# Scores of the two mixers: three products of rounded halves in place of one full-fp32 product

## The chip, the core and the metric

The kernel runs on one core of a Trainium2 chip. The metric is the time of one execution in device microseconds. Of the kernel before there are three runs: 2401.92, 2402.12 and 2405.55 us, a median of 2402.12. All times below are us unless marked ns. PE is the matrix engine (PEld its weight loads), DVE the vector engine, ACT the activation engine, POOL the general engine, and SP issues the weights' transfers.

## The reference

The model has two parts over one sequence of 256 tokens of width 1024. The first is a block of three attentions (block-sparse, dilated, memory), a gated merge and a convolved feed-forward. The second is a stack of two layers; each has a mixer and a layer of product-key experts (`peer`). The change is in the mixers alone. Cut to what matters there:

```python
h = rms_norm(x, norm1_g[l])
proj = h @ w_in[l]
q, k, v = ...                                   # 8 heads of 64
log_f = log_sigmoid(proj[..., F0:F1] + b_forget[l])
cum = cumsum(log_f)
logits = einsum("bhqd,bhkd->bhqk", q, k) * 64**-0.5
logits = logits + cum[q] - cum[k];  causal mask
y_att = softmax(logits) @ v
y_conv = silu(layer_norm(causal_dwconv(a * sigmoid(gate))))   # 31 taps
y_rnn = linear recurrence with gates, times gelu(gate_in)
x = x + concat(y_att, y_conv, y_rnn) @ w_out[l]
x = x + peer(rms_norm(x, norm2_g[l]), ...)
```

## The kernel before, in words

Weights come in as fp32 of 128x1024 (`wload`, L88). ACT rounds each to `hi` (fp32r, L102), and DVE or POOL makes the low half `lw` by a subtraction (L103). Activations are split in the same way (`split`, L106: ACT rounds, L108, and DVE subtracts, L109). A product of weights and activations is then three products of rounded halves, high x high, high x low and low x high: `gemm_n_unit` (L187, L188, L190; 512 columns) and `gemm_t` (L204 to L206; 256 columns). Attention is not done so: queries, keys, probabilities and values are plain fp32, and each of their products is one full-fp32 product, which the trace shows as two weight loads and two streams.

The mixer of layer `l` begins at L608. After the norm, the projections run as `proj_pair` (two weights into one PSUM tile of 512 columns). The queries and keys of heads 0 to 3 come first (`qk_proj`, L801) and ACT copies them to `qk` (L804); between the two projections stand the cumulative sum of the forget gates (L692, L693, which wait for `ff` of L678) and the recurrence's gates (L707). Then the values come (L822), and in the fill list the queries and keys of heads 4 to 7 (L841, L842) and the Gelu gate (L843).

`attention` (L224) is a generator in four stages for a pair of heads. Stage one makes the scores: for each half `t` of the queries and each head `j` one product L233 (64 rows, since a head is 64 wide; even heads sit in partitions 0 to 63, odd ones in 64 to 127), then `forget` adds the forget term (L814, bf16, 72 rows) and L238 adds the causal mask (bf16). For `t` = 0 a product has 128 columns, for `t` = 1 it has 256. Stage two: maximum (L248, DVE), Exp (L255, ACT), transposes (L274, PE), copies to SBUF (L276 ACT, L278 DVE). Stage three: the product with the values (L287) and the normalisation (L289). Stage four: transpose (L293) and split to `mh`, `ml`, the input of `w_out`.

`run_pairs` steps these generators in turn and puts fill between the stages: pairs 0 and 1 run together with the projections as fill, pair 2 with the first units of `w_out`, pair 3 (the last heads) with the other units. The convolution runs tap by tap on DVE (L732, `run_bg`), its layer norm is `ln_mean`, `ln_var`, `ln_out` (L759 to L790: L763, L773 and L786 on PE, L788 on DVE, then Silu on ACT, L789), and the recurrence is `rnn_roots`, `rnn_rsqrt`, `rnn_scan` (the long reciprocal is L741).

The order on each engine is not the order of the code: a scheduler places each instruction by its priority (`tc.high_priority`) and by when its inputs are expected. An engine then takes its instructions strictly in that order. An ACT function outside the loaded table needs an ACT_TABLE_LOAD, which stands in ACT's order too.

Of the kernel before, what the change touches and what calls it, by code (L numbers as in the profile page):

```python
# [10 lines left out]
F32 = mybir.dt.float32  # L11
F32R = mybir.dt.float32r
# [9 lines left out]
S = 256  # L22
# [28 lines left out]
def moba_peer_stack_kernel(ctx: ExitStack, tc: tile.TileContext, A, out):  # L51
    nc = tc.nc
    V, SC, GP, PE, SY = nc.vector, nc.scalar, nc.gpsimd, nc.tensor, nc.sync
# [52 lines left out]
    def split(hi, lo, ps, scale=None):  # L106
        if scale is None:
            SC.activation(hi, ps, AF.Copy)  # L108
            V.tensor_sub(lo, ps, hi.bitcast(F32))  # L109
        else:  # L110
            SC.activation(hi, ps, AF.Copy, scale=scale)  # L111
            V.scalar_tensor_tensor(lo, ps, scale, hi.bitcast(F32), op0=ALU.mult, op1=ALU.subtract)  # L112
# [111 lines left out]
    def attention(pool, heads, qT, kT, vv, full, dst, mask=None, cmul=None, extra=None):  # L224
        w0 = 256 if full else 128
        ws = [w0, 256]
        sp = [tmp_tile() for _ in range(2)]
        sps = [[sp[j][:, :w0] for j in range(2)], [sp[j][:, w0:w0 + 256] for j in range(2)]]
        for t in range(2):
            for j, h in enumerate(heads):  # L230
                o = sps[t][j]
                qs = qT(h)[:, t * 128:(t + 1) * 128]
                PE.matmul(o, qs, kT(h)[:, :ws[t]], start=True, stop=(full and extra is None))  # L233
                if extra is not None:
                    extra(o, h, ws[t])
                if not full:
                    if t == 0 or mask is None:
                        PE.matmul(o[:, t * 128:(t + 1) * 128], identb, trib, start=False, stop=True)  # L238
                    else:
                        PE.matmul(o, identb, mask, start=False, stop=True)  # L240
        yield
        mx = pool.tile([128, 2, 2], F32)
        for j in range(2):
            if full:
                V.tensor_reduce(mx[:, :, j], sp[j].rearrange("p (t k) -> p t k", t=2), axis=AX.X, op=ALU.max)
            else:
                for t in range(2):
                    V.tensor_reduce(mx[:, t, j:j + 1], sps[t][j], axis=AX.X, op=ALU.max)  # L248
        V.tensor_scalar(mx, mx, -SCALE, None, op0=ALU.mult)
        sm = pool.tile([128, 2, 2], F32)  # L250
        p = pool.tile([128, 2, 2, 256], F32)
        for t in range(2):
            for j in range(2):
                if cmul is None:
                    SC.activation(p[:, t, j, :ws[t]], sps[t][j], AF.Exp, scale=SCALE,  # L255
                                  bias=mx[:, t, j:j + 1], accum_out=sm[:, t, j:j + 1])
                else:
                    SC.activation(p[:, t, j, :ws[t]], sps[t][j], AF.Exp, scale=SCALE,
                                  bias=mx[:, t, j:j + 1])
                    V.scalar_tensor_tensor(p[:, t, j, :ws[t]], p[:, t, j, :ws[t]], 1.0,  # L260
                                           cmul[t], op0=ALU.mult, op1=ALU.mult,
                                           accum_out=sm[:, t, j:j + 1])
        V.reciprocal(sm, sm)
        on = pool.tile([128, 2, 2, 64], F32)
        pairs = [(k, t) for k in range(2) for t in range(2) if full or k <= t]
        n = len(pairs) * 128
        o0 = 0 if full else n
        ptss = []
        for j, h in enumerate(heads):
            pt = sp[j]  # L270
            pts = pool.tile([128, 512], F32)
            ptss.append(pts)
            for i, (k, t) in enumerate(pairs):
                PE.transpose(pt[:, i * 128:(i + 1) * 128], p[:, t, j, k * 128:(k + 1) * 128], ident)  # L274
            if j == 0:
                SC.copy(pts[:, :n], pt[:, :n])  # L276
            else:
                V.tensor_copy(pts[:, :n], pt[:, :n])  # L278
        yield
        for j, h in enumerate(heads):  # L280
            pt, pts = sp[j], ptss[j]
            ov = pt[:, o0:o0 + 128].rearrange("p (t d) -> p t d", t=2)
            for t in range(2):
                ks = [k for k in range(2) if (k, t) in pairs]
                for k in ks:
                    i = pairs.index((k, t))
                    PE.matmul(ov[:, t, :], pts[:, i * 128:(i + 1) * 128], vv(h, k),  # L287
                              start=(k == ks[0]), stop=(k == ks[-1]))
            V.tensor_mul(on[:, :, j], ov, sm[:, :, j, None].to_broadcast([128, 2, 64]))  # L289
        yield  # L290
        oT = sp[0]
        for t in range(2):
            PE.transpose(oT[:, t * 128:(t + 1) * 128], on[:, t].rearrange("p h d -> p (h d)"), ident)  # L293
        split(dst[0], dst[1], oT[:, :256])
# [34 lines left out]
    with ExitStack() as b1:  # L329
        ab = b1.enter_context(tc.tile_pool(name="b1", bufs=1))  # L330
# [276 lines left out]
    for l in range(L):  # L607
        with ExitStack() as mx:  # L608
# [20 lines left out]
            def proj_pair(i):  # L629
                ps = tmp_tile()  # L630
                for j in range(2):
                    wh, wl = wload(A["w2t"][l, 2 * i + j], 1024)
                    gemm_t(ps[:, j * 256:(j + 1) * 256], wh, wl, hh, hl)
                return ps.rearrange("p (a t) -> p a t", a=2)
# [161 lines left out]

            lo_on(GP)
            run_bg(8)
            qk = ab.tile([128, 8, S], F32)

            def qk_proj(i):  # L801
                for k in (0, 2):
                    s0 = 2 * i + 2 * k
                    SC.copy(qk[:, s0:s0 + 2], proj_pair(3 + i + k))  # L804
                    if k == 0:
                        forget_sum()
                        rnn_gates()
                    run_bg(10)

            def qf(s0):  # L810
                return lambda h: qk[(h % 2) * 64:(h % 2) * 64 + 64, s0 + h // 2, :]

            def forget(o, h, w):
                PE.matmul(o, sel[:, h, :], cumb[:, :w], start=False, stop=False)  # L814
# [12 lines left out]
            def pair_list(i, done):  # L827
                st = {}

                def unit(j):  # L830
                    if j == 0:
                        st["ps"] = acc_tile()
                    ps = st["ps"]
                    wh, wl = wload(A["w2t"][l, 2 * i + j], 1024)
                    gemm_t(ps[:, j * 256:(j + 1) * 256], wh, wl, hh, hl)
                    if j == 1:
                        done(ps.rearrange("p (a t) -> p a t", a=2))

                return [lambda: unit(0), lambda: unit(1)]

            fill = pair_list(4, lambda ps: SC.copy(qk[:, 2:4], ps))  # L841
            fill += pair_list(6, lambda ps: SC.copy(qk[:, 6:8], ps))  # L842
            fill += pair_list(7, lambda ps: SC.activation(gl, ps, AF.Gelu_apprx_tanh))  # L843
            fill = [lambda f=f: (f(), run_bg(12)) for f in fill]
            run_pairs([att(0), att(1)], fill, [2, 1, 1, 2], ahead=40)
# [325 lines left out]
```

## Time and profile before

| | |
|---|---|
| median of three runs | 2402.12 us |
| profiled execution | 2397.52 us |
| its span, first to last instruction | 2395.7 us |
| mean granted PE clock | 0.974 |
| PE busy | 2292.6 us, 96% |
| DVE / ACT / POOL busy | 67% / 52% / 28% |
| first mixer | 475 to 611 |
| second mixer | 1430 to 1566 |

The busy share counts a product until its modelled end, and products overlap, so durations on PE are not prices: the pitch between two starts is. The stretches in which the granted clock is 0.50 are given by the windows view. The two mixers are the same code with other weights, and their traces agree within a few tenths.

### The profile page before, as it was taken

To read this page: it belongs to the slowest core of one execution; us is meant where nothing else is said; L and a number is where in the kernel's file an instruction comes from. 1 tells how busy PE (TensorE), PEld (TensorE's weight loads), DVE (VectorE), ACT (ScalarE), POOL (GpSimd) and SP (SyncE) were. 2 spreads that over 40 slices of the span, in tenths; PEclk is the share of its full clock that TensorE was granted. 3 is DMA by queue.
4 is the path that set the end of the run, shared out by engine and by line. 5 is a ranking of instruction groups with operands and counts; after the bars stand their busy time and mean duration, and the time that the engine had idled before them with its cause. 6 is when DMAs were issued, how large, how long until landed. Compare 5 with 4: busy or idle time off the path is not lost. (4 is left out here: it accounts for less than half of the span.)

```text
span 2395.7 us, 37317 instructions
## 1 busy us (share of the span) xinstructions
PE 2292.6 (96%) x13972; PEld 2000.6 (84%) x13972; DVE 1611.9 (67%) x3269; ACT 1240.3 (52%) x1997; POOL 675.1 (28%) x279
## 2 busy tenths in 40 slices
PE   7799899989999999999999998999999999999998
PEld 6578688777898999998888877889899999888886
DVE  7832577767597667776666667759766777666665
ACT  5444466545444555555555544544455555555553
POOL 3436444334576111220000004468512122000000
PEclk9899899989999999999999998999999999999999
DMA  6424355524454555446666653445455555666664
GB/s 205 137 80 149 130 181 192 168 86 136 158 168 151 167 160 176 165 162 194 193 194 193 194 175 94 136 157 169 151 166 160 167 174 163 192 194 194 193 193 149
DMA packets 111934, 393.07 MB, mean 164 GB/s; under 512 B 13432, under 2 KB 14328, under 8 KB 111496
## 3 DMA queue, kind: packets, MB, share of 16 engines
q1 hardware_dynamic: 108288, 384.42, 50.6%
q10 hardware_dynamic: 3464, 6.26, 0.8%
q8 instruction: 110, 1.80, 0.3%
q14 instruction: 72, 0.59, 0.1%
HBM read 389.58 MB, written 1.05 MB: 163 GB/s over the span
## 5 line engine op out<-in xcount | busy, mean ns | idle before, releaser
L103 POOL TENSOR_TENSOR lw<-raw,hi 128x1024 fp32r<-128x1024 f32 (+1 forms) x275 | 674.9, 2459 | 1357.5 <-ACT hi L102 1159.4
L102 ACT ACTIVATE hi<-raw 128x1024 fp32r<-128x1024 f32 (+1 forms) x748 | 778.0, 1040 | 442.5 <-PE tmp L205 188.1
L103 DVE TENSOR_TENSOR lw<-raw,hi 128x1024 fp32r<-128x1024 f32 (+2 forms) x473 | 573.2, 1214 | 219.0 <-ACT hi L102 218.5
L204 PE MATMUL tmp<-th,hi 128*128 128x256 f32 x1696 | 494.6, 292 | 5.2 <-DVE th L112 3.3
L206 PE MATMUL tmp<-th,lw 128*128 128x256 f32 x1696 | 484.3, 286 | 9.8 <-POOL lw L103 9.8
L187 PE MATMUL acc<-hi,th 128*128 128x512 f32 x1248 | 491.0, 394 | 2.7 <-ACT pj L374 2.4
L188 PE MATMUL acc<-lw,th 128*128 128x512 f32 x1248 | 490.2, 393 | 2.6 <-POOL lw L103 1.9
L205 PE MATMUL tmp<-th,hi 128*128 128x256 f32 x1696 | 483.8, 285 | 0.3
L213 PE MATMUL tmp<-th,hi 128*128 128x512 f32 x1136 | 411.4, 399 | 0.9 <-DVE th L112 0.9
L190 PE MATMUL acc<-hi,th 128*128 128x512 f32 x1248 | 393.4, 391 | 0.0
L206 PEld LDWEIGHTS tmp<-th,lw 128*128 128x128 f32 x1696 | 327.4, 193 | 11.1 <-POOL lw L103 10.6
L204 PEld LDWEIGHTS tmp<-th,hi 128*128 128x128 f32 x1696 | 327.6, 193 | 8.0 <-DVE th L112 5.0
L205 PEld LDWEIGHTS tmp<-th,hi 128*128 128x128 f32 x1696 | 328.0, 193 | 1.2 <-DVE th L112 0.7
L187 PEld LDWEIGHTS acc<-hi,th 128*128 128x128 f32 x1248 | 235.8, 189 | 53.6 <-ACT pj L374 2.8
L188 PEld LDWEIGHTS acc<-lw,th 128*128 128x128 f32 x1248 | 236.1, 189 | 53.1 <-POOL lw L103 2.7
L215 PE MATMUL tmp<-th,lw 128*128 128x256 f32 x994 | 279.8, 281 | 0.0
L190 PEld LDWEIGHTS acc<-hi,th 128*128 128x128 f32 x1248 | 235.5, 189 | 49.6 <-issue 0.7
L111 ACT ACTIVATE th<-W 128x256 fp32r<-128x256 f32 x252 | 104.4, 419 | 284.5 <-PE acc L188 284.5
L213 PEld LDWEIGHTS tmp<-th,hi 128*128 128x128 f32 x1136 | 213.2, 189 | 41.8 <-DVE th L112 1.3
L215 PEld LDWEIGHTS tmp<-th,lw 128*128 128x128 f32 x994 | 188.9, 190 | 1.9
L112 DVE SCALAR_TENSOR_TENSOR th<-W,th 128x256 fp32r<-128x256 f32 x252 | 106.2, 424 | 111.5 <-PE acc L190 111.4
L982 DVE TENSOR_TENSOR tmp<-tmp,pb 128x256 f32<-128x256 f32 x98 | 42.4, 432 | 150.2 <-ACT pb L981 149.9
(339 smaller groups left out, 2472.1 us busy)
## 6 DMA issues: line engine op xcount, KB each, us to landing
raw<-in_u_dram SPq DMA_DIRECT2D x256, 512.0 KB, 3.7
raw<-in_v_dram SPq DMA_DIRECT2D x256, 512.0 KB, 3.5
raw<-in_w_up_dram SPq DMA_DIRECT2D x44, 512.0 KB, 3.6
raw<-in_w_in_dram SPq DMA_DIRECT2D x40, 512.0 KB, 3.5
raw<-in_w2t_dram SPq DMA_DIRECT2D x32, 512.0 KB, 3.9
raw<-in_wq_dram SPq DMA_DIRECT2D x32, 512.0 KB, 3.5
raw<-in_w_out_dram SPq DMA_DIRECT2D x24, 512.0 KB, 3.4
raw<-in_w_down_dram SPq DMA_DIRECT2D x22, 512.0 KB, 3.6
```

Of the source, the lines that this page charges most:

```text
L102: SC.activation(hi[:, :ncols], r, AF.Copy)
L103: lo.tensor_sub(lw[:, :ncols], r, hi[:, :ncols].bitcast(F32))
L111: SC.activation(hi, ps, AF.Copy, scale=scale)
L112: V.scalar_tensor_tensor(lo, ps, scale, hi.bitcast(F32), op0=ALU.mult, op1=ALU.subtract)
L187: PE.matmul(ps, lh, wh[:, sl], start=first, stop=False)
L188: PE.matmul(ps, lh, wl[:, sl], start=False, stop=False)
L190: PE.matmul(ps, ll, wh[:, sl], start=False, stop=last)
L204: PE.matmul(ps, wh[:, sl], ah[:, c, :], start=(c == 0), stop=False)
L205: PE.matmul(ps, wh[:, sl], al[:, c, :], start=False, stop=False)
L206: PE.matmul(ps, wl[:, sl], ah[:, c, :], start=False, stop=(c == KC - 1))
L213: PE.matmul(ps, wh[:, sl], a2[:, c].rearrange("p a b -> p (a b)"), start=(c == 0), stop=(c == KC - 1))
L215: PE.matmul(ps[:, :S], wl[:, sl], a2[:, c, 0], start=False, stop=False)
```

## The change

The score product takes its operands from two tiles, `qkh` (high) and `qkl` (low), both fp32r, which `split` fills from PSUM: ACT's copy becomes ACT's rounding and a DVE subtraction follows. In `attention`, three products of halves (high x high, high x low, low x high) accumulate where one full product stood. The first block's attentions pass single tiles and keep the full product.

```diff
@@ attention
-                qs = qT(h)[:, t * 128:(t + 1) * 128]
-                PE.matmul(o, qs, kT(h)[:, :ws[t]], start=True, stop=(full and extra is None))
+                q, k = qT(h), kT(h)
+                ts = slice(t * 128, (t + 1) * 128)
+                prods = [(q[a][:, ts], k[b][:, :ws[t]]) for a, b in ((0, 0), (0, 1), (1, 0))] \
+                    if isinstance(q, tuple) else [(q[:, ts], k[:, :ws[t]])]
+                for n, (qs, ks) in enumerate(prods):
+                    PE.matmul(o, qs, ks, start=(n == 0),
+                              stop=(n == len(prods) - 1 and full and extra is None))
@@ the mixers
-            qk = ab.tile([128, 8, S], F32)
+            qkh = ab.tile([128, 8, S], F32R)
+            qkl = ab.tile([128, 8, S], F32R)
+
+            def qk_split(s0, ps):
+                split(qkh[:, s0:s0 + 2], qkl[:, s0:s0 + 2], ps)
+
...
-                    SC.copy(qk[:, s0:s0 + 2], proj_pair(3 + i + k))
+                    qk_split(s0, proj_pair(3 + i + k))
...
-                return lambda h: qk[(h % 2) * 64:(h % 2) * 64 + 64, s0 + h // 2, :]
+                def at_head(h):
+                    r = slice((h % 2) * 64, (h % 2) * 64 + 64)
+                    return qkh[r, s0 + h // 2, :], qkl[r, s0 + h // 2, :]
+                return at_head
...
-            fill = pair_list(4, lambda ps: SC.copy(qk[:, 2:4], ps))
-            fill += pair_list(6, lambda ps: SC.copy(qk[:, 6:8], ps))
+            fill = pair_list(4, lambda ps: qk_split(2, ps))
+            fill += pair_list(6, lambda ps: qk_split(6, ps))
```

The scheduler also orders the mixers anew. In the changed kernel, L233 is L237, L238 is L243, L255 is L260, L276 is L281, L741 is L746, L743 is L748, L773 is L778, L789 is L794 and L814 is L827.

On PE, in the scores of the last pair of heads, this stood before (`qk` feeds the scores, `mh` and `ml` feed `w_out`):

```order
L233 MATMUL tmp<-qk 128x128
L814 LDWEIGHTS sel
L814 MATMUL tmp<-cumb,sel 128x128
L238 LDWEIGHTS identb
L238 MATMUL tmp<-trib,identb 128x128
L188 MATMUL acc<-lw,mh 128x512
L187 MATMUL acc<-hi,mh 128x512
L814 LDWEIGHTS sel
L814 MATMUL tmp<-cumb,sel 128x256
```

And this stands there now:

```order
L237 MATMUL tmp<-qkh 128x128
L187 MATMUL acc<-hi,mh 128x512
L237 MATMUL tmp<-qkl,qkh 128x128
L188 MATMUL acc<-lw,mh 128x512
L187 MATMUL acc<-hi,mh 128x512
L237 MATMUL tmp<-qkh,qkl 128x128
L188 MATMUL acc<-lw,mh 128x512
L827 LDWEIGHTS sel
L827 MATMUL tmp<-cumb,sel 128x128
L190 MATMUL acc<-hi,ml 128x512
```

Products of `w_out` have moved in between the three products of one score. Over this pair, from its first score to its last mask, 12 of them stand now and 7 stood before; between the last mask and the transposes of the probabilities 12 now and 9 before, between those transposes and L287 2 now and 8 before, and up to L293 3 now and 5 before.

On ACT, at the end of the mixer (the last pair's probabilities `p`, and the convolution's output `yc`), before:

```order
L255 ACTIVATE p,sm<-tmp,mx 128x128 x2
L255 ACTIVATE p,sm<-tmp,mx 128x256 x2
L102 ACTIVATE hi<-raw 128x1024
L789 ACT_TABLE_LOAD
L789 ACTIVATE yc<-yc,pv 128x256 x2
L276 COPY pts<-tmp 128x384
L108 ACTIVATE mh<-yc 128x512
```

Now:

```order
L794 ACT_TABLE_LOAD
L794 ACTIVATE yc<-yc,pv 128x256
L260 ACT_TABLE_LOAD
L260 ACTIVATE p,sm<-tmp,mx 128x128 x2
L260 ACTIVATE p,sm<-tmp,mx 128x256
L794 ACT_TABLE_LOAD
L794 ACTIVATE yc<-yc,pv 128x256
L260 ACT_TABLE_LOAD
L260 ACTIVATE p,sm<-tmp,mx 128x256
L108 ACTIVATE mh<-yc 128x512
L281 COPY pts<-tmp 128x384
```

The first Silu has moved ahead of the four Exp and the second between the third and the fourth, each with a table load on either side.

On DVE, ahead of the first scores, where the low half of the keys of heads 0 to 3 is made, now:

```order
L745 TENSOR_SCALAR rq<-th 128x512
L737 SCALAR_TENSOR_TENSOR acc<-yp,pv,acc 128x256
L746 RECIPROCAL rq<-rq 128x512
L109 TENSOR_TENSOR qkl<-tmp,qkh 128x512
L747 TENSOR_SCALAR av<-rq 128x512
L748 TENSOR_SCALAR tg<-th 128x512
```

The new subtraction stands right behind the reciprocal, where before the next steps of the recurrence stood. The other one for heads 0 to 3 (the queries) has taken the place of a tap two rows ahead of the last steps of `ff`. On POOL and SP nothing has moved.

## Rows read from the trace of the kernel before

**Rows 1.** The page, parts 1 and 4: busy time; the last chain's shares by engine.
```profile
PE 2292.6 (96%) x13972; PEld 2000.6 (84%) x13972; DVE 1611.9 (67%) x3269; ACT 1240.3 (52%) x1997; POOL 675.1 (28%) x279
...
PE 33%; POOL 0%; DVE 0%; ACT 0%; DVEq 0%; issue 0%; POOLq 0%; ACTq 0%
```

**Rows 2.** PE's waits, first mixer, 475 to 616: total, times, longest.
```profile
PE tmp L692 <- DVE ff L678: 6.4, 1, 6.4
...
PE tmp L233 <- ACT qk L804: 1.1, 1, 1.1
PE acc L206 <- POOL lw L103: 0.8, 1, 0.8
```

**Rows 3.** PE in order of time, scores of pair 2: start, duration, engine, line.
```profile
566.68 0.28 PE L205 MATMUL acc<-th,hi 128*128 128x256 f32 x1
566.80 0.28 PE L206 MATMUL acc<-th,lw 128*128 128x256 f32 x1
567.01 0.48 PE L233 MATMUL tmp<-qk 64*128 64x128 f32 x2
567.42 0.39 PE L204 MATMUL acc<-th,hi 128*128 128x256 f32 x1
...
569.45 0.70 PE L233 MATMUL tmp<-qk 64*128 64x256 f32 x2
570.07 0.38 PE L204 MATMUL acc<-th,hi 128*128 128x256 f32 x1
```

**Rows 4.** PE in order of time, from the last pair's last mask on.
```profile
591.32 0.33 PE L238 MATMUL tmp<-trib,identb 128*128 128x128 bf16 x1
...
593.47 0.39 PE L187 MATMUL acc<-hi,mh 128*128 128x512 f32 x1
593.70 0.39 PE L188 MATMUL acc<-lw,mh 128*128 128x512 f32 x1
...
594.84 0.82 PE L274 MATMUL tmp<-ident,p 128*128 128x128 f32 x6
595.41 0.71 PE L190 MATMUL acc<-hi,ml 128*128 128x512 f32 x2
...
598.17 1.55 PE L287 MATMUL tmp<-vn,pts 128*128 128x64 f32 x12 [0.65 <-ACT pts L276]
...
600.76 0.38 PE L293 MATMUL tmp<-ident,on 128*128 128x128 f32 x2
```

**Rows 5.** ACT and DVE in order of time: copies, reciprocal and subtraction of 128x512.
```profile
526.69 3.34 DVE L741 RECIPROCAL rq<-rq 128x512 f32<-128x512 f32 x1
...
530.59 0.57 ACT L804 COPY qk<-tmp 128x512 f32<-128x512 f32 x1
...
598.02 0.63 ACT L108 ACTIVATE mh<-yc 128x512 fp32r<-128x512 f32 x1
...
599.35 0.68 DVE L109 TENSOR_TENSOR ml<-yc,mh 128x512 fp32r<-128x512 f32 x1
```

**Rows 6.** ACT (and one DVE row) in order of time, behind the last scores.
```profile
593.03 0.36 ACT L255 ACTIVATE p<-tmp,mx 128x128 f32<-128x128 f32 x1
...
593.38 0.47 ACT L255 ACTIVATE p<-tmp,mx 128x256 f32<-128x256 f32 x1
...
594.80 0.75 DVE L788 TENSOR_TENSOR yc<-yc,tmp 128x256 f32<-128x256 f32 x2 [1.44 <-PE tmp L786]
...
595.36 1.28 ACT L789 ACT_TABLE_LOAD   x1
596.66 1.09 ACT L789 ACTIVATE yc<-yc,pv 128x256 f32<-128x256 f32 x2
597.66 0.46 ACT L276 COPY pts<-tmp 128x384 f32<-128x384 f32 x1
```

**Rows 7.** Windows: stretch, length, busy (count) of PE, PEld, DVE, ACT, POOL; granted clock, DMA.
```profile
514.70:524.90 10.20, 6.29 (x19) 4.57 (x20) 9.98 (x32) 1.93 (x5) 0.00 (x0) 0.50 0.12 33
586.40:593.20 6.80, 6.80 (x19) 4.05 (x19) 3.46 (x18) 0.59 (x4) 0.00 (x0) 0.50 0.50 158
```

## The prediction

> **What bounds the kernel now.** I read the page's first and fourth parts first, then PE's waits in the first mixer, then PE and ACT in order of time where the scores are made. PE is busy 96% of the span, and the chain that ended last is PE's wherever its steps are named [rows 1]. So time that PE gains or loses in a mixer is kept, unless PE waits there for something else. In the first mixer it waits 6.4 us for the forget gates (DVE), 1.1 us for the ACT copy of keys at the first scores, 0.8 us for one low weight half from POOL, and 0.65 us at L287 for the last heads' probabilities [rows 2, 4]. The second mixer repeats the pattern.
>
> The scores are small: 2 mixers x 4 head pairs x 2 heads x 2 query halves = 32 products with 64 rows. What matters is what stands around one. The L206 product at 566.80 streams for 0.12, as the pitch from 566.68 shows, so it ends at 566.92; the score product starts at 567.01, 0.09 later, and the next L204 starts 0.41 after that [rows 3]. For 256 columns instead of 128 the 0.41 becomes 0.62: 128 columns more cost 0.21, so 128 columns stream for 0.21 and 0.20 is fixed (a weight load of about 0.11 with nothing beside it, and 0.09 before the next row count). The L204 behind it then takes 0.39 where others take 0.28: another 0.11 for its own weights [rows 3]. **A visit to the 64-row form costs 0.09 + 0.11 + 0.09 + 0.11 = 0.40 us beside its streaming**, and about 0.29 where a bf16 mask (L814) follows, whose weights load faster. Full fp32 alone isn't the reason: six full-fp32 transposes with 128 rows and the step to the next product take 0.57 together, under 0.10 each [rows 4].
>
> **The change part by part.**
>
> *Products on PE.* Each score product of full fp32 becomes three rounded ones. Counted in PE's order, a visit is a run of score products with nothing else between. Per layer there were 14 visits (6 end at a mask), now 24 (8 end at a mask): the scheduler puts other products between the three. Before: 6 x 0.29 + 8 x 0.40 = 4.9. After: 8 x 0.29 + 16 x 0.40 = 8.7. So +3.8 per layer. Streaming: 8 products of 0.21 and 8 of 0.42 were 5.0; now 24 of 256 columns at 0.12 (the pitch of the same form with 128 rows) are 2.9, and 24 of 128 columns cost between 0.06, half of that, and 0.11, if the weight load sets the pitch. I take 0.08, since some stand alone and some follow one another: 1.9. Streaming changes by -0.2 (-0.7 to +0.5). PE: **+3.6 per layer**.
> No row shows a rounded product with 64 rows. Its ends are the streaming alone, with no price for the visit (the first rival), and the 0.62 of a full product each; I take the measured price of the visit, which its neighbours pay whatever the type.
>
> *The first scores.* They waited for L804 [rows 2]. Now ACT's rounding copy takes about 0.06 more (0.63 against 0.57), and the low part is a DVE subtraction of 0.68 behind it [rows 5]. Three products of high parts can run meanwhile, some 0.3. A subtraction also stands in place of one conv tap ahead of the forget gates' last steps, for which PE waits anyway: 0.2. So 0.06 + 0.68 - 0.3 + 0.2 = **+0.65 per layer**. On DVE the subtraction of the keys stands behind the long reciprocal of L741, which ended at 530.03, before ACT's copy began at 530.59, so it waits for ACT and not for DVE; behind it stand the steps of the recurrence, whose end is needed only much later.
> A layer's other two subtractions, for the heads 4 to 7, lie beside PE's streaming of other weights: 36 products at 0.12 stand in PE's order between the transposes that go before them on ACT and the first score that wants a low half. Without that cover they would cost up to 0.63 + 0.68 = 1.3 each; I cost them at nothing.
>
> *The last heads.* Here ACT's order matters more. Before, the four exponentials of the last pair stood together and the convolution's two Silu after them, with one table load. Now Silu and Exp alternate: Silu, three Exp, Silu, one Exp, with a load of 1.28 ahead of each, three more per layer. From the last mask at 591.32 to L287 at 598.17 it took 6.85 us [rows 4]. After: the first convolution multiply on DVE (about 0.4) and its semaphores (about 0.4), then on ACT load 1.28, Silu 0.50, load 1.28, Exp 0.35 + 0.35 + 0.47, load 1.28, Silu 0.50, load 1.28, Exp 0.47, the rounding copy of yc 0.53, the copy of probabilities 0.46: 8.75 [rows 5, 6]; with the lead 9.5, of which 0.2 run before the last mask: 9.3, or +2.5. Then two products of w_out fewer stand between L287 and L293 (0.23 each [rows 4]), so L293 comes **+2.0 later** after the last score. PE cannot hide it, since 14 products and the transposes (some 4 us) stand in the 9.3. Five products of w_out that used to fill this time now stand ahead of the last score: 5 x 0.23 = **+1.15**.
>
> *What is absorbed.* The 0.8 wait for POOL lies behind the first scores, so lateness up to there can vanish in it, if POOL isn't late itself; its weights wait for buffers that PE frees. Between 0 and 0.75; I take 0.4.
>
> *The clock.* PE's granted clock is 0.50 (1.2 GHz) between 586.4 and 593.2, in the midst of the last scores and without a wait ahead of it; it is 0.50 too from 514.7, in the 6.4 us wait, to 524.9 [rows 7]. I take the stretch at the last scores to stay as long as it is. If it went, each layer would gain back about 2.4, half of the 4.9 from 586.4 to the last mask; if one more of 6.8 us fell on dense work, it would cost half, 3.4.
>
> *Sum.* Per layer 3.6 + 0.65 + 2.0 + 1.15 - 0.4 = 7.0; two layers +14.0. The profiled execution took 2397.5 (2395.7 of span and 1.8 around it), so 2411.5 by it. The median of the runs is 4.6 above that execution; on the median the forecast is **2416 us**.
>
> **The rivals.**
> *The price belongs to the full-fp32 product, not to the row count.* Then the 28 visits of before lose 28 x 0.40 = 11.2, streaming gives 0.4, and the waits and moved work of the two layers add 2 x (0.65 + 2.0 + 1.15 - 0.4) = 6.8: 2402.1 - 11.6 + 6.8 = 2397, faster. It decides at the 64-row runs. Against it: transposes and L287 of full fp32 pay no such gap [rows 4], and the gap stands on both sides of the 64-row product. The Trainium skill (TensorEngine Tiling (Array Packing), Tiling Modes) says that a change of tiling mode drains the engine; the 0.09 on either side agrees. Chance 0.07.
> *The tail and the fragments are hidden.* If Exp and Silu find time while PE has work after all, and the visits overlap because the two heads sit in different row halves, half of the 14 stays: 2404 to 2409. For it: the order puts the two heads' products side by side at the first scores. Against: 128-row products stand between most visits, and at the last pair ACT has nothing but its own chain to do. Chance 0.13.
> *The clock falls longer.* The last scores have 11 visits instead of 4, and behind them PE would wait some 5 us; the 6.4 us wait went with half speed [rows 2, 7]. One more stretch per layer gives 2416 + 6.8 = 2423, two 2430. Chance 0.22.
> *A switch of tables costs more than its load.* If ACT had to run empty at each switch and that took as long as the load, the four of the chain would add 2 x 4 x 1.28 = 10: 2426. Against it: Silu follows 0.02 after the load's end [rows 6]. The Trainium skill (ScalarE: Activation LUTs, What ACT_TABLE_LOAD costs) gives about 2.66 us for a switch, 1.28 of it the load and the rest a drain, by which it would be 11; the row's 1.28 agrees for the load, and no drain shows in it. Chance 0.01.
>
> **How the numbers follow.** The forecast holds 0.57 (2410 to 2420). About 0.2%, 4.8 us, is what a measurement of this kernel can tell from no change. The first rival is faster, or in part the same: faster 0.05, same 0.02; of the second about half lies under 2406.9: same 0.07; slower 0.86. The range leaves out the first rival's end and the two-stretch end: 2404 to 2427.
>
> **What would show it.** The products of L237 are 96 in the mixers, and each visit in the last scores still has 0.09 ahead and 0.4 around it. L794 and L260 have three more table loads per layer, and PE waits about 5 us for the last pair's probabilities where it waited 0.65. The wait at the first score gets some 0.7 longer in all. PE's gaps elsewhere (before L165 and L204) stay. I am wrong if rounded products follow 128-row ones without a gap, if the last wait stays under 2 us, or if the difference lies outside the two mixers.

## The result: slower, 2434 us, and the profile after

The changed kernel takes 2433.68 us (2432.20 to 2433.75) against 2402.12, a ratio of 1.0128, 95% interval [1.0109, 1.0146]. Run once more later it took 2435.14, 1.0131 [1.0105, 1.0158]. I had said 2416 and at most 2427: the direction was right, the size was not. The loss is 31.6 us, where I had 14.

The page's parts 1 and 4 read as before [rows 1], PE's chain first:

```profile
PE 2317.0 (95%) x14004; PEld 2016.3 (83%) x14004; DVE 1614.0 (66%) x3277; ACT 1247.6 (51%) x2003; POOL 672.1 (28%) x279
...
PE 33%; POOL 0%; DVE 0%; ACT 0%; issue 0%; DVEq 0%; POOLq 0%; ACTq 0%
```

Where the time went is best read between marks that both traces have. Starts of PE's products in the first mixer, counted from its first L165, and by how much each comes later after the change (the second mixer in the last column):

| mark (line after) | before | after | later | later, second mixer |
|---|---|---|---|---|
| first score (L237) | 51.34 | 51.48 | +0.1 | -1.3 |
| statistics of the convolution (L768), w_out under way | 96.36 | 96.92 | +0.6 | -0.6 |
| last score (L237) | 109.20 | 121.03 | **+11.8** | **+10.8** |
| last pair's L292 | 118.30 | 132.72 | +14.4 | +13.4 |
| last pair's L298 | 120.90 | 136.57 | +15.7 | +14.6 |
| next stage (L165) | 135.49 | 151.52 | +16.0 | +15.0 |

The two mixers lose 31.0 together. What lies outside differs too, without a changed instruction in it: the first mixer began 7.1 us later in this profile, and 1.8 came back elsewhere. Over all kernels of this study, that start lay between 0.1 and 13.4 us behind the one of before, 9.9 in the second profile of the same changed kernel; so stages are compared from the mixer's start, and a total within some microseconds by medians only.

Of the 11.8, 11.3 arise between L768 and the last score, and so do 11.4 in the second mixer. The mark L768 is not quite steady: seven products of `w_out` stood ahead of it before, three stand there now, and each takes 0.23. A steadier stretch is that from the last pair's first score, which has 24 products of `w_out` ahead of it in every kernel here, to its last mask: 17.81 now (591.48 to 609.29), 7.26 before (584.06 to 591.32). Of this difference 1.5 are the third pair's L292, which stands behind that first score now and stood ahead of it before.

The windows of the changed kernel (stretch, length, busy time and count of PE, PEld, DVE, ACT, POOL, then granted clock, DMA share, GB/s) answer to [rows 7]:

```profile
593.60:614.10 20.50, 19.64 (x47) 11.75 (x47) 6.19 (x25) 5.69 (x11) 2.87 (x2) 0.50 0.24 78
617.50:624.30 6.80, 6.17 (x23) 5.55 (x24) 3.05 (x6) 2.53 (x6) 0.00 (x0) 0.50 0.00 1
1563.00:1583.50 20.50, 19.65 (x47) 11.75 (x47) 6.19 (x25) 5.68 (x11) 2.87 (x2) 0.50 0.24 78
```

In both mixers PE runs at half clock (1.2 GHz) for 20.5 us where it was 6.8 [rows 7], and again for 6.8 us behind its wait in the tail. The rows of PE in order of time show visits to the 64-row form at the full clock (first pairs and third pair), and what they become in the stretch:

```profile
547.85 0.38 PE L237 MATMUL tmp<-qkh 64*128 64x256 f32 x1
548.16 0.51 PE L190 MATMUL acc<-hi,th 128*128 128x512 f32 x1
548.59 0.39 PE L237 MATMUL tmp<-qkh 64*128 64x256 f32 x1
...
575.39 0.28 PE L206 MATMUL acc<-th,lw 128*128 128x256 f32 x1
575.60 0.32 PE L237 MATMUL tmp<-qkh 64*128 64x128 f32 x1
575.85 0.39 PE L204 MATMUL acc<-th,hi 128*128 128x256 f32 x1
...
594.73 0.69 PE L298 MATMUL tmp<-ident,on 128*128 128x128 f32 x2 [0.86 <-DVE on L294]
...
600.59 0.58 PE L237 MATMUL tmp<-qkh 64*128 64x256 f32 x1
601.10 0.79 PE L187 MATMUL acc<-hi,mh 128*128 128x512 f32 x1
601.82 0.58 PE L237 MATMUL tmp<-qkl,qkh 64*128 64x256 f32 x1
602.33 0.79 PE L188 MATMUL acc<-lw,mh 128*128 128x512 f32 x1
603.06 0.58 PE L237 MATMUL tmp<-qkh,qkl 64*128 64x256 f32 x1
603.57 0.79 PE L187 MATMUL acc<-hi,mh 128*128 128x512 f32 x1
```

At the full clock the rounded product starts 0.09 behind the end of L206 (575.39 + 0.12), the next starts 0.25 later and takes 0.39 instead of 0.28: just the visit that I had priced for the full fp32 product [rows 3], and with a rounded one it is the same. A score of 256 columns and one product of 512 columns take 0.74 together at the full clock (547.85 to 548.59) and 1.23 in the stretch (600.59 to 601.82), so half clock costs this mixture 0.4 of its time, not half. The last two heads made four visits before; now they make eleven, with twelve products of w_out between them instead of seven.

PE's waits from 482 to 624 (total, times, longest) answer to [rows 2]:

```profile
PE tmp L697 <- DVE ff L683: 6.5, 1, 6.5
...
PE tmp L279 <- ACT p L260: 3.2, 1, 3.2
...
PE tmp L237 <- ACT qkh L108: 1.1, 1, 1.1
PE tmp L298 <- DVE on L294: 0.9, 1, 0.9
PE acc L206 <- POOL lw L103: 0.5, 1, 0.5
PE tmp L237 <- DVE qkl L109: 0.3, 1, 0.3
```

The 3.2 at L279 took the place of 0.65 at L287, and 0.9 at L298 (for the third pair, at 594.73 above) is new. ACT's own rows in the tail show why the first is there, answering to [rows 6]:

```profile
609.82 1.28 ACT L794 ACT_TABLE_LOAD   x1 [1.86 <-DVE yc L793]
611.12 0.60 ACT L794 ACTIVATE yc<-yc,pv 128x256 f32<-128x256 f32 x1
611.72 1.28 ACT L260 ACT_TABLE_LOAD   x1
613.02 0.37 ACT L260 ACTIVATE p<-tmp,mx 128x128 f32<-128x128 f32 x1
...
614.30 1.28 ACT L794 ACT_TABLE_LOAD   x1
615.60 0.60 ACT L794 ACTIVATE yc<-yc,pv 128x256 f32<-128x256 f32 x1
616.21 1.28 ACT L260 ACT_TABLE_LOAD   x1
617.51 0.47 ACT L260 ACTIVATE p<-tmp,mx 128x256 f32<-128x256 f32 x1
```

Silu and Exp alternate, four loads of 1.28 where there was one. From the last mask at 609.29 to L292 at 619.68 it took 10.4, against 6.85 [rows 4].

### The profile page after: what moved, and what is told of

Its sections match the earlier page's. It is cut to its first block, busy times and chain, and to the rows that moved or that the text cites. A ratio compares the mean times of both kernels' runs of the same rounds, so it can differ in the third digit from the quotient of the medians.

```text
span 2432.0 us, 37389 instructions
## 1 busy us (share of the span) xinstructions
PE 2317.0 (95%) x14004; PEld 2016.3 (83%) x14004; DVE 1614.0 (66%) x3277; ACT 1247.6 (51%) x2003; POOL 672.1 (28%) x279
## 5 line engine op out<-in xcount | busy, mean ns | idle before, releaser
L206 PE MATMUL tmp<-th,lw 128*128 128x256 f32 x1696 | 482.1, 284 | 9.8 <-POOL lw L103 9.8
L206 PEld LDWEIGHTS tmp<-th,lw 128*128 128x128 f32 x1696 | 325.1, 192 | 11.1 <-POOL lw L103 10.6
```

The lines of the kernel that those rows point to most:

```text
L206: PE.matmul(ps, wl[:, sl], ah[:, c, :], start=False, stop=(c == KC - 1))
```

## The experiments

Theory: the single 64-row products among the last heads' 128-row ones hold PE at half clock, and that is what I missed. Rivals: the order of the last pair does it, whatever the rows; the visits alone; ACT's tail; the rounding and its splits. Ratios are to the kernel before, run on the same chip beside each group: 2400.1 (first four), 2400.2 (next four), 2404.9 (last three).

**All scores with 128 rows.**
```
- qkh = ab.tile([128, 8, S], F32R)
+ kh = ab.tile([128, 4, S], F32R)
+ qzh = ab.tile([128, 4, 2, S], F32R)
...
+     V.memset(z[(1 - r) * 64:(2 - r) * 64, :, r, :].bitcast(F32), 0.0)
...
+     split(qzh[p, s0:s0 + 2, r], qzl[p, s0:s0 + 2, r], ps[p])
```


> The changed kernel, but a head's query lies in 128 rows with its other 64 set to zero, and its key comes with the neighbour's: all 96 rounded products of the scores have 128 rows, and the order on every engine is that of the changed kernel; the same scores are computed. Clock theory (in each mixer the last pair's stretch at half speed, 20.5 us, comes from the 64-row products standing singly among 128-row ones): the gaps around them go (24 x 0.4 us a layer) and the stretch is as short as before the change, 6.8 us; 2434 - 2 x (9.6 + 7) is about 2401, and with the dearer splits 2400 to 2410. Order theory (the longer half-speed stretch comes from the order and the waits of the last pair, whatever the rows): the gaps go, the stretch stays over 15 us, 2414 to 2420. Tail theory (the ScalarE chain behind the last mask costs most): over 2420.

Measured 2424.11, 1.0086 [1.0061, 1.0112]. Between L768 and the last score the loss fell from 11.3 to 2.5 and 2.7, and the stretch there to 6.8 us (600.2 to 607.0): the clock theory's signs. But the order did not stay as I had meant: 14 products of w_out stand ahead of L768 here, three in the changed kernel, so 2.5 of that gain (11 x 0.23) are the mark's. From the last pair's first score to its last mask, over the same products in nearly the same order, it is 11.22 (597.80 to 609.03) instead of 17.81. The time is far above the clock theory's 2400 to 2410. The 13 visits of the first three pairs are gone, yet w_out begins 96.1 us into the first mixer, as in the changed kernel (96.2), because PE waits 3.3 us more for ACT and DVE there; that the splits by halves of rows cause these waits is likely and not shown. The tail stayed (1.9 up to L292, 1.25 to L298), and this profile began its first mixer 13.4 late.

**The last pair in full fp32.**
```
+ if s0 % 4 == 2:
+     split(qkh[:, s0:s0 + 1], qkl[:, s0:s0 + 1], ps[:, :1])
+     SC.copy(qkf[:, s0 // 4:s0 // 4 + 1], ps[:, 1:])
...
+ if h >= 6:
+     return qkf[r, s0 // 4, :]
```


> The changed kernel, but the scores of the last two heads of each mixer (6 and 7) are full fp32 products again, from an unsplit copy: 4 visits to the 64-row form instead of the many single ones in the last pair, ScalarE's tail (Silu and Exp in turn) as in the changed kernel. Clock theory: the half-speed stretch at the last scores is back at 6.8 us, and what is left over the kernel before is the tail (about 4 us a layer), the first score (under 1) and a few visits (1 to 1.5): 2402 + 2 x 6 to 7, so 2412 to 2417. Visits theory (the stretch is not the cause, only the 0.4 us of each visit): 3 visits a layer less, 2434 - 2.4, about 2431. Tail theory: 2430 or more, since the tail is unchanged.

Measured 2434.07, 1.0138 [1.0117, 1.016]: far from what my theory said. But the edit moved the order as well: the third pair, still rounded, now stands singly among the products of the gate, ten visits instead of six, and there the clock fell:

```profile
574.90:585.10 10.20, 10.20 (x35) 7.95 (x36) 3.28 (x10) 1.31 (x2) 2.34 (x1) 0.50 0.25 84
...
595.40:605.60 10.20, 9.99 (x29) 6.34 (x29) 4.77 (x22) 1.25 (x2) 0.00 (x0) 0.50 0.34 104
```

Up to L768 6.0 us are lost in the first mixer, and 7.5 in the second, that weren't lost in the changed kernel. It doesn't decide between the theories; it shows that the place isn't bound to the last pair, and that an experiment has to hold the order. It also speaks against a simple count of visits: the last pair makes four, as before the change, and its stretch is 10.2, not 6.8.

**Silu behind the last Exp.**
```
+ def ln_silu():
+     for c in range(2):
          SC.activation(yc[:, c], yc[:, c], AF.Silu, scale=P(f"lg{l}", c), bias=P(f"lb{l}", c))
      split(mh[:, 4:6], ml[:, 4:6], yc)
...
- run_pairs([att(3)], units[4:7], 1, ahead=40)
+ run_pairs([att(3)], [lambda: None, lambda: (ln_silu(), units[4]()), units[5]], 1, ahead=40)
+ units[6]()
```


> The changed kernel, but the Silu of the gate is emitted behind the Exp of the last heads, so ScalarE changes its table 29 times in the program instead of 31, and the last heads' probabilities come without a change between them; the products of the scores stay as they are and stand singly among the products of w_out (22 visits a layer instead of 24). Tail theory: the time from the last mask to the last products of the probabilities falls from 10.4 us to about 7.5; 2434 - 2 x 3 to 4, so 2426 to 2428, more if the chain is most of the loss. Clock theory: the stretch of 20.5 us at half speed stays, 2425 to 2431; if the stretch falls below 10 us here, the time is under 2420 and neither the rows nor the single visits were what set it.

Measured 2426.09, 1.0108 [1.0085, 1.0131]. That fits both theories' times. The scheduler still put one Silu ahead of the Exp, so the probabilities still waited for two loads; the tail up to L292 stayed 2.2 above before, and my edit tested that theory only in part. Of the 3.4 us a layer that it gained, 2.9 came between L768 and the last score, where two visits and three products of w_out fewer stood and the stretch was 17.1 in both mixers.

**No w_out between the last scores.**
```
-         lambda: (ln_out(), units[3]()), lambda: None]
+         lambda: ln_out(), lambda: None]
...
- run_pairs([att(3)], units[4:7], 1, ahead=40)
+ def behind_scores():
+     with tc.issue_after(last_mask["m"].ins):
+         units[3]()
+ run_pairs([att(3)], [lambda: (behind_scores(), units[4]()), units[5], units[6]], 1, ahead=40)
```


> The changed kernel, but the twelve products of w_out that stand between the last pair's scores are issued behind the pair's last mask, so nothing of 128 rows comes between the last scores but the decay's two products, the masks and the transposes; 20 visits a layer instead of 24, the rounded 64-row products as they are, and the tail's wait filled with products of w_out; table changes 25. Clock theory: the scores themselves are over in about 8 us instead of 20; if the mixture with w_out's products held the clock down, the stretch is 10 us or less and the time is 2434 - 2 x (7 + 1.6 + 2 to 4), so 2408 to 2414. Rows theory (64-row products hold the clock down whatever lies between): the stretch moves with the scores and stays as long for w_out's products behind them; 2420 to 2428. Tail theory: the wait for the probabilities is filled, 2434 - 2 x 4, so about 2426.

Measured 2401.85, 1.0011 [0.9996, 1.0027]: nearly all of the loss is gone, with the same rounded 64-row products. The windows of the two stretches:

```profile
588.30:598.50 10.20, 10.20 (x33) 7.16 (x33) 5.08 (x23) 2.10 (x9) 0.56 (x1) 0.50 0.33 104
1544.00:1554.20 10.20, 10.20 (x33) 7.16 (x33) 5.09 (x23) 2.10 (x9) 0.57 (x1) 0.50 0.33 104
```

They are 10.2 us instead of 20.5. From L768 to the last score, with as many products of w_out between as before, it is 1.6 longer than before, and Exp stands together again, so PE no longer waits for it: L292 follows the last score only 0.7 later than before. The time is below every forecast. The two mixers give back 26.8 of the 32.3 us between the two profiled executions, a little over the 25 that the clock theory had at most; 5.2 lie ahead of the first mixer, where nothing differs.

**128 rows for the last pair alone.**
```
+ if s0 == 2:
+     split(qkh[:, 2:3], qkl[:, 2:3], ps[:, :1])
+     for r in range(2):
+         p = slice(r * 64, r * 64 + 64)
+         split(qzh[p, r:r + 1], qzl[p, r:r + 1], ps[p, 1:])
...
+ if h >= 6:
+     return (qkh[:, 7, :], qkl[:, 7, :]) if s0 else (qzh[:, h - 6, :], qzl[:, h - 6, :])
```


> The changed kernel, but of the last two heads of each mixer alone (6 and 7) the query lies in 128 rows with the other 64 zero; PE's order is that of the changed kernel, product for product, and the same scores are computed. Clock theory: between the start of w_out and the last score the loss falls from 11.3 us a layer to the 2.5 of the kernel with 128 rows throughout, and the half-speed stretch from 20.5 us to 6.8; 2434 - 2 x 8.8, so 2414 to 2419. Order theory (the stretch belongs to the order of the last pair, whatever the rows): the stretch stays over 15 us and only the visits go, 10 x 0.4 us a layer: 2426 or more.

Measured 2420.32 (2413.90 to 2422.45), 1.008 [1.0056, 1.0104], just above the clock theory's range and below the order theory's; the profiled execution took 2413.9. From the last pair's first score on PE's order is that of the changed kernel, product for product; a few products of the gate and of L768 ahead of it stand elsewhere. The window of the last scores:

```profile
586.70:595.50 8.80, 7.42 (x54) 6.27 (x53) 6.80 (x21) 2.33 (x4) 2.35 (x1) 1.00 0.38 121
```

And PE's rows of the same products as shown above of the changed kernel:

```profile
590.11 0.44 PE L298 MATMUL tmp<-ident,on 128*128 128x128 f32 x2 [1.38 <-DVE on L294]
...
592.48 0.28 PE L237 MATMUL tmp<-qkh,qzh 128*128 128x256 f32 x1
592.61 0.40 PE L187 MATMUL acc<-hi,mh 128*128 128x512 f32 x1
592.84 0.29 PE L237 MATMUL tmp<-qkl,qzh 128*128 128x256 f32 x1
592.96 0.39 PE L188 MATMUL acc<-lw,mh 128*128 128x512 f32 x1
593.20 0.28 PE L237 MATMUL tmp<-qkh,qzl 128*128 128x256 f32 x1
593.31 0.40 PE L187 MATMUL acc<-hi,mh 128*128 128x512 f32 x1
```

Same order, and now the clock is 1.00 through all the last scores: a score and a w_out product take 0.36 (592.48 to 592.84) instead of 1.23. From the first score of the pair to its last mask it is 8.63 us (586.79 to 595.42) where the changed kernel needs 17.81 (591.48 to 609.29). From L768 to the last score the loss is 1.8 and 2.0 instead of 11.3 and 11.4, of which 0.9 are four products of w_out that stand ahead of the mark here. That excludes the order by itself, and the rounding: in this order it is the row count of 24 products, 12 a layer. (With 64 rows the order counts too, as the run without w_out between the last scores shows.) The half-speed stretch did come later (602.5 to 612.7), in the tail behind PE's wait, which is still there (5.3 us at L279). Of the 8 us a layer that are left, 6.2 lie behind the last mask and 1.7 and 2.0 ahead of it, where five products of w_out and four of L791 stand that stood behind it before.

The kernel with 128 rows throughout has the same products in its last pair and took 11.22 for them, with 6.8 us at half clock, where this one took 8.63 with none. So 6.8 us at half clock cost 2.6 there, again 0.4 of it. And since neither has a 64-row product there, the row count doesn't explain why a stretch of 6.8 begins in the one and none in the other.

**The kernel before, no w_out between the scores.** The edit of the fourth run, full fp32.

> The kernel before the change, with w_out's products moved behind the last pair's last mask as in the run without w_out between the scores, the full fp32 products left. If the move only takes away what the change added, it does nothing here: 2398 to 2402. If it also fills the wait of 5 us for the last heads' probabilities, which the kernel before has too: 2 x 2 to 4 us faster, 2392 to 2397. The difference from the changed kernel with the same move (2401.9) is the price of the rounded products by themselves: by the visits (6 more a layer at 0.4 us) and the first score (0.7), 2 x 3.1, about 6 us.

Measured 2394.51, 0.9977 [0.9963, 0.9991]: faster than before, at the time of the second reading but not for its reason: the kernel before waits 0.65 for the last heads' probabilities [rows 4], not 5. In the profile the mixers end 0.9 and 3.7 earlier than before's, but they stand 1.6 and 1.4 ahead at the first score already, where nothing is edited yet; and in the second mixer the stretch is 3.4 instead of 6.8. What made this kernel faster is not shown. Against 2401.85 with rounded products, these cost 7.3 us in this order (I had said about 6), the longer stretch included.

**Grouped, no w_out between.**
```
+ for a, b in ((0, 0), (0, 1), (1, 0)):
+     for j, h in enumerate(heads):
+         PE.matmul(sps[t][j], q[a][:, ts], k[b][:, :ws[t]], start=(a + b == 0), stop=False)
```


> The changed kernel with w_out's products behind the last scores, and in addition the products of the two heads of a pair issued in turn, all high by high, then the cross products: 14 visits to the 64-row form a layer, as many as before the change, instead of 20. Visits theory: 2401.9 - 2 x 6 x 0.4, about 2397. If the clock alone counts, and it is as good as it gets already: 2400 to 2403. Over 2405 if the first score's wait for both heads' splits costs more than the visits give.

Measured 2398.97, 0.9993 [0.9979, 1.0007]; 2.9 of the expected 4.8 us came. The intervals of the two runs overlap, and the stretch is shorter too, 6.8 us with five visits in the last scores, so this doesn't price the visits by themselves. By its median it is the best form of the rounded scores here, the same as the kernel before, and 4.5 us behind it with the same move.

**The changed kernel again.**

> The changed kernel itself once more, as a control: 2431 to 2437. If the half-speed stretch of 20.5 us in the last scores is the same at every execution, it is 17 to 21 us here in both mixers; if it was an accident of one profile, it is shorter in one of them. The time until the first mixer, in which nothing is changed, lay 7.1 us apart in the two profiles; if that is chance, it lies elsewhere here.

Measured 2435.14, and the stretches to the digit:

```profile
597.00:617.50 20.50, 19.64 (x47) 11.75 (x47) 6.17 (x25) 5.70 (x11) 2.87 (x2) 0.50 0.24 78
1566.40:1586.90 20.50, 19.66 (x47) 11.72 (x47) 6.22 (x25) 5.64 (x10) 2.92 (x2) 0.50 0.25 78
```

They are no accident of a profile. The start of the first mixer is: 9.9 us behind before's here, 7.1 in the first profile.

**The kernel before, each score cut in three.**
```
- PE.matmul(o, qs, kT(h)[:, :ws[t]], start=True, stop=(full and extra is None))
+ for c0, c1 in zip(cuts, cuts[1:]):
+     PE.matmul(o[:, c0:c1], qs, kT(h)[:, c0:c1], start=(c0 == 0), stop=(full and extra is None))
```


> The kernel before the change, full fp32 scores without any split, but each score's product is cut into three along the keys (44, 44 and 40 columns, and 88, 88 and 80): as many products as in the changed kernel, and on PE the last pair in nearly the changed kernel's order, single products of 64 rows between w_out's of 128; 28 visits a layer. If it is the breaking up of the scores that costs (visits and clock) and not the rounding: a half-speed stretch of 15 us or more at the last scores, and 2420 to 2440. If it is something in the rounded products or in the split: the stretch stays near 6.8 us, and only the visits (14 more a layer at up to 0.4 us) and ScalarE's order show: 2400 to 2416.

Measured 2443.66, 1.0175 [1.0152, 1.0199]: full fp32 scores, nothing rounded, and slower than the changed kernel. The time fits the breaking up of the scores, but the clock fell elsewhere than I said: not at the last scores, but 10.2 us long at the third pair (from 576.2), as in the run with the last pair in full fp32, and again in the tail:

```profile
576.20:586.40 10.20, 10.20 (x38) 8.27 (x38) 3.73 (x11) 0.85 (x1) 2.34 (x1) 0.50 0.18 51
613.70:623.90 10.20, 8.30 (x28) 7.20 (x29) 3.57 (x7) 4.06 (x7) 0.00 (x0) 0.50 0.13 36
```

Part of the loss is the pieces themselves, 4.3 us by the first pair's transposes, and 10.9 of the 21.5 us a layer are lost by the last pair's first score, where the changed kernel had lost next to nothing. So a loss of this size needs no rounding, but it is not the same loss. The last pair makes nine visits here, between the same products as in the changed kernel, and the clock is 1.00 throughout: 11.58 from its first score to its last mask (595.13 to 606.71). That speaks against the theory that the visits alone set the stretch; its place I can't foretell.

**The kernel before, no w_out between, and 128 rows for heads 4 to 7.**
```
+ def q_pad(ps):
+     for r in range(2):
+         p = slice(r * 64, r * 64 + 64)
+         SC.copy(qz[p, :, r], ps[p])
...
+ if h >= 4:
+     return qk[:, s0 + h // 2, :] if s0 else qz[:, h // 2 - 2, h % 2, :]
```


> The kernel before the change with w_out's products behind the last scores (2394.5), and in addition the queries of the last four heads of each mixer in 128 rows with the other 64 zero, full fp32: half of the scores need no change of form. By the visits (7 of 14 a layer go, 0.3 to 0.4 us each): 2394.5 - 2 x 2 to 2.8, so 2389 to 2391. If the copies by halves of rows or the zeros cost as much as that: 2394 to 2398.

Measured 2390.56, 0.9946 [0.9927, 0.9965], the fastest: 11.6 us under the kernel before by its first median, 14.4 by its runs beside. Its interval and that of the same kernel without the 128 rows just touch. In the profile the mixers end 4.8 and 5.9 earlier than before's, of which 1.6 and 1.2 stand at the first score already. In the last scores and behind them the clock stays full:

```profile
583.50:604.00 20.50, 19.29 (x112) 15.93 (x112) 9.88 (x34) 10.40 (x20) 7.05 (x3) 1.00 0.35 104
```

**Grouped alone.** The edit of the seventh run, w_out's products left between.

> The changed kernel with the products of a pair's two heads issued in turn, w_out's products still between the last scores: 18 visits a layer instead of 24, eight of them single products of the last pair between w_out's products. Visits theory: 2434 - 2 x 6 x 0.4, about 2429. Clock theory, if the single visits of the last pair are what holds the clock down: the stretch stays over 15 us, 2424 to 2432; if it shortens to 10 us or less here, the time falls under 2422.

Measured 2428.51, 1.0092 [1.0063, 1.0121]. Both theories' times hold it. Nine visits are left in the last scores, and the stretches are between those of five and eleven, though one of them shorter than I had set for the clock theory:

```profile
597.70:611.40 13.70, 13.70 (x36) 8.23 (x37) 4.85 (x14) 2.27 (x3) 1.95 (x1) 0.50 0.22 71
1567.10:1584.20 17.10, 16.70 (x43) 10.27 (x44) 6.72 (x23) 3.85 (x5) 2.37 (x1) 0.50 0.23 65
```

Side by side, the last pair's visits to the 64-row form and the half-clock stretch that begins in its scores, both mixers:

| kernel | visits | stretch, us | median, us |
|---|---|---|---|
| before, no w_out between, 128 rows for heads 4 to 7 | 0 | none | 2390.6 |
| changed, 128 rows for the last pair | 0 | none | 2420.3 |
| changed, all 128 rows | 0 | 6.8, 6.8 | 2424.1 |
| before | 4 | 6.8, 6.8 | 2402.1 |
| before, no w_out between | 4 | 6.8, 3.4 | 2394.5 |
| changed, last pair in full fp32 | 4 | 10.2, 10.2 | 2434.1 |
| changed, grouped, no w_out between | 5 | 6.8, 6.8 | 2399.0 |
| changed, no w_out between | 7 | 10.2, 10.2 | 2401.9 |
| before, each score cut in three | 9 | none | 2443.7 |
| changed, grouped | 9 | 13.7, 17.1 | 2428.5 |
| changed, Silu late | 9 | 17.1, 17.1 | 2426.1 |
| changed, both times | 11 | 20.5, 20.5 | 2433.7, 2435.1 |

In two of these kernels, the last pair in full fp32 and the scores cut in three, the clock had been at half for 10.2 us in the third pair already (10 and 11 visits there, six in the changed kernel). These two don't fit. In the others more visits went with a longer stretch, but for the 6.8 us that one has without any.

## Why the prediction was too low

**The step that failed is the clock**: "I take the stretch at the last scores to stay as long as it is." It is 20.5 us in both mixers where it was 6.8, and a second one of 6.8 lies behind PE's wait in the tail. My third rival named both places, but gave them one or two more stretches of 6.8 (2423 or 2430), a chance of 0.22, and a range that left its two-stretch end out; the last scores alone have 13.7 more. Of the 17.81 from the last pair's first score to its last mask, 15.7 lie at half clock (593.6 to 609.29), 0.9 of them in a wait; before it was 4.9 (586.4 to 591.32). At 0.4 for each us, as the two comparisons above have it, the longer stretch costs 0.4 x (14.8 - 4.9), by this estimate some 4 us a layer. My rule of half the time would have made it more. The run with 128 rows in the last pair bears the sum out: over the same products it needs 9.2 less, of which some 4 are its eleven visits and over 5 the clock.

**Two small terms were missing in the same place.** The 0.9 at L298, where PE waits for the third pair's division on DVE; and four short products of L791 that stand ahead of the last mask now (607.26 and 608.49, two each), 0.1 apiece. My own terms up to the last mask, 3.6 + 0.65 + 1.15 - 0.4, were 5.0. With 0.9 + 0.4 and the clock's 4 they make 10.3; measured are 10.9 in the first mixer and 9.9 in the second.

**The visit was priced rightly**: 0.09, 0.25 to the next start, 0.39 behind. It is a price of the change of form, not of full fp32: at the full clock a rounded score of 256 columns and its neighbour take 0.74 with 64 rows and 0.36 with 128. My first rival would have been faster; it is excluded by these rows.

**The tail was longer than I said, in part by the clock.** L292 stands 10.4 behind the last mask, where I had 9.3 (6.85 before). ACT's chain from the first load to the end of the copy took 9.1 of it (609.82 to 618.96) instead of my 8.75, since a Silu or an Exp with a load behind it takes 0.1 more; and at the end PE had two products of w_out at half clock to do. From L292 to L298 it is 3.84, where I had 2.60 less 0.46: the stretch from 617.5 to 624.3 lies on L292 and the w_out products behind it, and twelve products of L292 show 2.65 busy instead of 1.55 [rows 4]. In the six profiles in which PE waits 3.2 in one piece for the last heads' probabilities this step takes 3.84, and in the five kernels whose longest wait there is 1.2 or less it takes 2.59 to 2.62. So L298 is 4.8 later after the last mask instead of the 2.0 that I had. PE's wait was 3.2 and not 5, because the products ahead of it ran at half clock and filled the time; in the run with 128 rows for the last pair, where they ran at the full clock, it is the 5.3. Three more table loads a layer are there. That a switch costs more than its load is not borne out: Silu at 611.12 follows 0.02 behind the load's end, and Exp at 613.02 the same. The Trainium skill (ScalarE: Activation LUTs, What ACT_TABLE_LOAD costs) gives about 2.66 us for a switch with its drain; these rows show 1.28 and the 0.02, so the measurement decides.

**The start was about what I said.** At L768 it was +0.6 in one mixer and -0.6 in the other, but four products of w_out (0.9) have moved from ahead of this mark to behind it, so the same work is 1.5 and 0.3 later. I had 0.65 - 0.4 and three more visits, about 1.4. The second mixer is better because PE came 1.3 earlier out of the wait for the forget gates, as in most other kernels' second mixers here.

In sum, first mixer: 10.9 up to the last mask, 3.5 more to L292, 1.25 more to L298 and 0.4 to the next stage: 16.05 for the 16.0 measured; I had 7.0.

**What stays open.** That in the changed kernel's order the row count of the last pair's products makes the long stretch is shown (17.81 against 8.63, in both mixers). That its length goes with the number of visits holds for most of the kernels in the table and fails for two: four visits with 10.2 us, and nine with none. Why the visits bring half clock, by their pauses of 0.2 us or by the half of the rows that does nothing, these runs don't tell apart: PE's busy time shows 19.64 of 20.50, since a product counts as busy until its modelled end. Nor can I say where a stretch begins; two kernels had it one pair earlier, and one had 6.8 us of it without a 64-row product. And the 7 to 10 us by which the changed kernel's first mixer began later in both its profiles, with nothing changed ahead of it, are not explained.

## What to carry to other kernels

Splitting a small product into several doesn't only multiply its own cost: it gives the scheduler more pieces to put between others, and each piece that changes the row count on PE pays the change twice. Where many of them fall into one stretch, price that stretch at half clock as well (here 0.4 us for each us of it), and expect half clock again behind a wait that the new order brings. Keep such products together (issue the filler behind them), or give them the neighbours' row count with zeros: both together made the kernel before 0.5% faster, with no split at all.

## What the runs showed of the hardware

- In the last scores the clock was at half for none to 20.5 us. With the products and their order the same, it was 20.5 with 64 rows in 24 of them, 12 a layer, and none with 128.
- Half clock cost 0.4 of the time spent at it, not half, where 64-row scores and products of 512 columns take turns: 1.23 against 0.74.
- Rows of zeros cost PE nothing that shows: a score of 256 columns with 128 rows, half of them zero, went through in 0.13 (592.48 to 592.61), and the last scores in 8.63 us where the 64-row ones took 17.81.
- Stages in which no instruction differs moved by up to 13 us between profiles; the runs of the kernel before alone spread from 2397.8 to 2409.2.
